# A hybrid convolution and S5 encoder block on one core: the convolution moved in between the last SSM batches, and the out-projection's halves in the other order

## The chip, the cores and the metric

One core of one Trainium2 chip runs the whole block. The metric is the device time of the kernel in microseconds (us); the kernel before takes 2246.47 us, the median of three runs.

## What is computed

The input is one sequence of 2048 vectors of 1024 channels, in front of which 16 learned meta tokens are put. The block is, with everything in float32:

```
p = rms_norm(h) @ w_in          # columns: 512 conv value, 512 conv gate, 512 S5 input
conv = silu(layer_norm(depthwise_conv31(value * sigmoid(gate)) + conv_b))
s5   = glu(gelu(S5(input) + D * input))   # 32 groups x 16 channels, 64 complex states, 2 directions
h = h + concat(conv, s5) @ w_out
h = h + relu(rms_norm(h) @ w_ff1)**2 @ w_ff2
out = rms_norm(h) without the meta positions
```

## The kernel before

The 2048 tokens are cut into 16 tiles; tile t holds the tokens 16c + t, c = 0..127, and four tiles make a block (blk = 0..3). A large matrix product is done in split precision: each operand is a high and a low part, and `mm3` (L150) issues three 512-column matmuls (L151, L152, L153) for one product. So a "unit" of the in-projection, one gate, value or u output of 128 channels for one block, is 8 x 3 = 24 matmuls.

The order of the program is the order of priority for a scheduler that fills each engine's list: an instruction written earlier goes first if its operands can be there, and later ones fill the gaps. The stages in that order are:

1. In-projection of blocks 0 and 1 and the parameters of the SSM, up to about 236 us.
2. The SSM, `ssm_run(b)` for b = 0..15 (L722), each batch a pair of groups. In a batch TensorE forms `v` from the loaded `u` (8 matmuls, L733); DVE turns it with phasors (`r`, `zi`), scans it in both directions (L751, L752) and turns it back (`s`, `st`); TensorE then makes `y` from `u` with `mt` and from `st` with `pc` (16 matmuls, L766, L769), and ACT writes it to DRAM (`ydr`). `ssm_prep(b + 3)` (L644) makes the matrices of a later batch: `pb`, its transposes `tr_wb` and `wb`, `pc`, the local kernel `k` and, by way of DRAM (`gdr`), `mt`. The in-projection of blocks 2 and 3 (`do_u`, `do_gv`, L283 and L296) is written after or among the batches and fills TensorE between their steps.
3. The convolution, `conv_quad(q)` for q = 0..15 (L824), each 32 channels. SP loads a `u8` of 260 KB (L829) from `vdr`, where the gated value was written, and four `cb` of 192 KB (L833), the banded filter; each `cb` meets three 128-column matmuls (L835), and DVE adds the bias into four blocks `cv` (L840). There are two `u8` and six `cb` buffers. All these loads stand in the one in-order queue of SP.
4. The out-projection. `s5_out(blk)` (L878) loads `y`, forms gelu, the GLU (`glu`, 48 matmuls per block) and `wout_mm(0, blk)`; then `ln_out(blk)` (L907) takes the layer norm of `cv` (16 BN_STATS at L911 over all blocks, a normalise, transposes `tr_ln`, `lzz`, a split `zc` whose low part is made on POOL) and `wout_mm(1, blk)` (L853) multiplies by the other half of w_out. Each `wout_mm` reads the residual from DRAM and writes it back: the first half x to `pdr`, the second `pdr` to `hdr`.
5. The feed-forward part, in which TensorE never rests, to the end.

Four slots of 16 KB per partition, `zslot` (L76), hold the normalised blocks z (high and low parts of two at a time) and later the split w_out (`woh`, `wol`) and the FFN's z2.

Of the kernel before, what the change touches and what calls it, by code (L numbers as in the profile page):

```python
# [1 line left out]

# [35 lines left out]
def hymba_kernel(ctx, tc, x, meta, norm_mix_g, w_in, conv_w, conv_b, conv_ln_g, conv_ln_b,  # L38
# [72 lines left out]
    def rsqrt(src, n, scale, name):  # L111
        """1 / sqrt(scale * src + eps), src [P, n]."""
        a, y, t, u = (consts.tile([P, n], F32, tag=f"rs_{q}{n}", name=f"rs{q}_{name}", bufs=2) for q in "aytu")
        tsc(a, src, scale, ALU.mult, EPS, ALU.add)
        rsqrt_steps(y, a, t, u)
        return y

    def rsqrt_steps(y, a, t, u):
        """y = a^-1/2: a guess from the exponent, a Newton step, a step of third order"""
# [4 lines left out]
        stt(u, t, -3.0, y, ALU.add, ALU.mult)         # -2 y  # L124
# [29 lines left out]

    with ExitStack() as es2:
# [45 lines left out]
        # ---------------- in-projection  # L201
# [22 lines left out]
        def load_split(src, name, hot=True, meta=False):  # L224
            """src: [1024, 128] of a weight -> hi / lo tile [P, 2, (k, col)]; the meta tokens' part of the product."""
# [21 lines left out]
        def meta_mm(r, n, name):  # L247
            """[(quarter of k, token), n]: parts of the product of the meta tokens"""
# [8 lines left out]
        def meta_cols(name):  # L257
            """[P, 16], in PSUM: the columns of the meta tokens"""
# [24 lines left out]
        def do_u(half, j, w=None, blks=None, ps=None):  # L283
            if w is None:
                w = u_weights(half, j, meta=(half == 0))
            for blk in blks or (2 * half, 2 * half + 1):
# [4 lines left out]
                with tc.high_priority():  # L291
                    st = stage(j, blk, umeta, f"stu{j}_{blk}")
                    S.copy(out=st[:, :, 1:W - 1], in_=ps.rearrange("p (s c) -> p s c", s=4))
                    flush(S, st, j, blk, udr)

        def do_gv(half, j, by_block=False):  # L296
# [25 lines left out]
            for f, blk in ([(f, blk) for blk in blks for f in (gate, value)] if by_block  # L322
                           else [(f, blk) for f in (gate, value) for blk in blks]):
                f(blk)

        def cmul(o, a, b, t0, t1):
            """complex product of APs given as (re, im)"""
# [7 lines left out]
        with (tc.tile_pool(name="pp", bufs=1, reuse_waits="tile") as PP,  # L335
# [4 lines left out]
            # ---------------- SSM parameters, [(dir, p), g]  # L340
# [31 lines left out]
            def sincos(so, co, th):  # L372
# [16 lines left out]
                # quadrant  # L389
# [25 lines left out]
            def pview(o, nr, n):  # L415
                """[P, part, batch, g, n]; parts: re, im, then sums"""
# [3 lines left out]
            pha, phb = pview(448, 3, 10), pview(508, 4, 13)      # Q^(13 a), Q^b  # L420
# [8 lines left out]
            def ssm_load():  # L429
# [14 lines left out]
                # C  # L444
# [16 lines left out]
                # D on the diagonal  # L461
# [7 lines left out]
            def ssm_params():  # L469
# [12 lines left out]
                # f = (lambda - 1) / lam  # L482
# [18 lines left out]
                # powers of lambda  # L501
# [12 lines left out]
                # rho = |lambda|^16  # L514
# [4 lines left out]
                # Q = unit phasor of lambda^16 (conjugate for the reverse direction)  # L519
# [50 lines left out]
                # the forward states are read two columns on: Q^-2  # L570
# [18 lines left out]
            # ---------------- convolution  # L589
# [25 lines left out]
            do_u(0, 0, uw[0], (0,), ps0)  # L615
            do_u(0, 1, uw[1], (0,))
# [3 lines left out]
            for j in range(2):  # L620
                do_u(0, j, uw[j], (1,))
            load_cols()
            ssm_load()
            do_u(0, 2)
            do_u(0, 3)
# [3 lines left out]
        with (tc.tile_pool(name="pb", bufs=1, reuse_waits="tile") as PB,  # L629
# [14 lines left out]
            def ssm_prep(b):  # L644
# [4 lines left out]
                def pv(o, nr, n):  # L649
                    """[P, part, g, n]"""  # L650
# [5 lines left out]
                def outer(o_re, o_im, a, b4, la, lb, on=V):  # L656
                    """complex products of a and b4, laid out by la and lb, from three real ones"""
# [17 lines left out]
                # W_b: [(h, s'), g, half of h, ri, (dir, p)]  # L675
# [41 lines left out]
                # phasor tables  # L717
# [60 lines left out]

            for j in range(4):
                do_gv(0, j, by_block=(j == 3))  # L780
# [6 lines left out]
            for j in range(2):  # L787
                do_u(1, j, uw[j], (2,))
# [3 lines left out]
            for j in range(2):  # L792
                do_u(1, j, uw[j], (3,))
            for b in range(16):
# [10 lines left out]
        # ---------------- convolution, S5 output, out-projection  # L805
        gB = consts.tile([P, D], F32, tag="gvec", name="gffn", bufs=1)
        SP.dma_start(gB, norm_ffn_g[0].partition_broadcast(P))
        with tc.tile_pool(name="p3", bufs=1, reuse_waits="tile") as P3:
# [3 lines left out]
            convb = t3([P, 512], "convb")  # L812
            SP.dma_start(convb, conv_b[0].partition_broadcast(P))

            cv = [t3([P, 4, 512], f"cv{blk}") for blk in range(4)]
# [3 lines left out]
            def hl_tile(name):  # L819
                if not hlp:  # L820
                    hlp.append(es3.enter_context(tc.tile_pool(name="p3b", bufs=1, reuse_waits="tile")))
                return hlp[0].tile([P, 2, 512], F32R, tag="hl", name=name, bufs=9)

            def conv_quad(q):  # L824
                """channels 32 q .. 32 q + 31"""
                j = q // 4
                ps = ks_ps(f"cv{q}", [P, 4, NT, 8])
                u8 = t3([P, 4, W], f"u8_{q}", bufs=2, tag="u8")
                SP.dma_start(u8, dap(vdr[j], (q % 4) * 32 * NT * W, [[W, P], [P * W, 4], [1, W]]))  # L829
                for i in range(4):  # L830
                    g8 = 4 * (q % 4) + i
                    cb = t3([P, 384], f"cb{q}_{i}", tag="cb", bufs=6)
                    SP.dma_start(cb, dap(edr[j], g8 * 8 * 504, [[504, 8], [8, 16], [1, 384]]))  # L833
                    for m in range(3):
                        T.matmul(ps[:, i].rearrange("p t c -> p (t c)"), u8[:, i, 2 - m:2 - m + P], cb[:, ts(m, P)],  # L835
# [256 lines left out]
```

## Time and profile before

| | us |
|---|---|
| median of 3 runs (lowest, highest) | 2246.47 (2242.87, 2249.4) |
| span of the profiled execution | 2244.0 |
| PE busy / DVE busy / ACT busy / POOL busy | 2143.7 / 1311.7 / 552.5 / 158.3 |
| SSM batches, first v to last v | 236.7 to 450.5 |
| end of the in-projection | about 496 |
| convolution, first to last matmul | 496.2 to 582.4 |

The profile gives no time for the execution beside its span; the span lies between the lowest and the median of the runs. The busy time of PE is 96% of the span, but that is an average: it holds a feed-forward stage of 1400 us at 100%. The stages to read for this change lie between 236.7 and 850 us.

### The profile page before, as it was taken

Reading aid. Unit: us, or ns where it says so; the run is one execution under the profiler, and the core shown is the slowest. Engines: PE = TensorE matmul, PEld = TensorE weight load, DVE = VectorE, ACT = ScalarE, POOL = GpSimd, SP = SyncE. Lnnn points to the kernel's source line nnn. Section 1 sums busy time; section 2 is a strip of 40 time slices with the busy share of each in tenths; the row PEclk is TensorE's granted clock in tenths of the full one; section 3 lists DMA queues with packets and bytes.
Section 4 is the critical chain, followed back from the end, with each engine's and each line's share of the span. In section 5 each row is a group of like instructions: output and inputs, shape, how many; then the busy total and the mean of one; then the engine's idle time right before and its main releaser. Section 6 shows DMA issues by size and latency. Waiting matters only on the chain.

```text
span 2244.0 us, 26522 instructions
## 1 busy us (share of the span) xinstructions
PE 2143.7 (96%) x10508; PEld 1750.8 (78%) x10508; DVE 1311.7 (58%) x2399; ACT 552.5 (25%) x886; POOL 158.3 (7%) x240
## 2 busy tenths in 40 slices
PE   7989888898999999999999999999999999999998
PEld 5767777776777778888888888888888888888886
DVE  6866799952676555554444454469544444554456
ACT  5323222230233222112212211234122122112212
POOL 1031344400002100000000000000000000000000
PEclk9999999999999999999999999999999999999999
DMA  6245344356543574111111111225111111112102
GB/s 189 92 163 184 114 116 126 115 172 201 163 140 114 201 260 135 47 38 62 52 38 57 47 47 40 64 66 186 59 59 55 38 57 48 47 39 63 50 19 75
DMA packets 189955, 215.37 MB, mean 96 GB/s; under 512 B 19789, under 2 KB 153433, under 8 KB 189320
## 3 DMA queue, kind: packets, MB, share of 16 engines
q1 hardware_dynamic: 174696, 199.89, 28.4%
q10 hardware_dynamic: 13856, 9.54, 1.4%
q0 software_dynamic: 1280, 4.26, 0.5%
q8 instruction: 82, 1.34, 0.3%
q14 instruction: 41, 0.34, 0.0%
HBM read 168.65 MB, written 45.01 MB: 95 GB/s over the span
## 4 chain that ended last, share of the span: by engine, by line
PE 70%; DVE 15%; DMA 6%; issue 3%; ACT 1%; POOL 0%; SPq 0%; ACTq 0%; DVEq 0%; POOLq 0%
PE f L151 19%; PE f L153 19%; PE f L152 19%; DMA cb<-edr 3%; PE wo L151 2%; PE wo L153 2%; PE wo L152 2%; DVE zo L752 1%; DVE acc L62 1%; DVE s L45 1%; DVE r L45 1%; DVE zo L751 1%; PE cv L835 1%; DVE k L663 1%; DVE st L45 1%
## 5 line engine op out<-in xcount | busy, mean ns | idle before, releaser
L45 DVE TENSOR_TENSOR acc<-acc,f 128x512 f32<-128x512 f32 x480 | 327.1, 687 | 252.3 <-PE f L153 252.3
L151 PE MATMUL f<-w,hid 128*128 128x512 f32 x1024 | 399.8, 390 | 0.6 <-DVE acc L45 0.5
L151 PE MATMUL f<-z2h,w 128*128 128x512 f32 x1024 | 399.3, 390 | 0.0
L152 PE MATMUL f<-w,hid 128*128 128x512 f32 x1024 | 398.9, 390 | 0.0
L153 PE MATMUL f<-z2h,w 128*128 128x512 f32 x1024 | 398.7, 389 | 0.0
L153 PE MATMUL f<-w,hid 128*128 128x512 f32 x1024 | 398.6, 389 | 0.0
L152 PE MATMUL f<-z2l,w 128*128 128x512 f32 x1024 | 398.6, 389 | 0.0
L45 DVE TENSOR_TENSOR rr<-rr 128x512 f32<-128x512 f32 x128 | 88.6, 693 | 352.2 <-ACT rr L990 352.2
L134 ACT CAST w<-raw 128x1024 fp32r<-128x1024 f32 x128 | 131.3, 1048 | 584.0 <-PE f L153 566.0
L151 PEld LDWEIGHTS f<-w,hid 128*128 128x128 f32 x1024 | 192.1, 188 | 46.8 <-DVE acc L45 3.7
L153 PEld LDWEIGHTS f<-w,hid 128*128 128x128 f32 x1024 | 192.2, 188 | 40.3
L151 PEld LDWEIGHTS f<-z2h,w 128*128 128x128 f32 x1024 | 192.2, 188 | 40.1 <-ACT z2h L134 0.2
L153 PEld LDWEIGHTS f<-z2h,w 128*128 128x128 f32 x1024 | 192.2, 188 | 39.9
L152 PEld LDWEIGHTS f<-z2l,w 128*128 128x128 f32 x1024 | 192.2, 188 | 39.7
L152 PEld LDWEIGHTS f<-w,hid 128*128 128x128 f32 x1024 | 192.2, 188 | 38.1
L990 ACT ACTIVATE rr<-f 128x512 f32<-128x512 f32 x128 | 76.5, 599 | 412.6 <-PE f L153 412.6
L135 DVE TENSOR_TENSOR w<-raw,w 128x1024 fp32r<-128x1024 f32 x128 | 154.0, 1222 | 10.8 <-ACT w L134 10.7
L135 DVE TENSOR_TENSOR hid<-rr,hid 128x512 fp32r<-128x512 f32 x128 | 88.1, 689 | 40.5 <-ACT hid L134 40.4
L134 ACT CAST hid<-rr 128x512 fp32r<-128x512 f32 x128 | 79.1, 619 | 57.5 <-DVE rr L45 57.5
L835 PE MATMUL cv<-cb,u 128*128 128x128 f32 x384 | 59.6, 295 | 18.0 <-DMA cb<-edr 14.6
L45 DVE TENSOR_TENSOR xo<-xo,wo 128x512 f32<-128x512 f32 x64 | 43.8, 684 | 52.9 <-PE wo L153 52.5
L835 PEld LDWEIGHTS cv<-cb,u 128*128 128x128 f32 x384 | 48.9, 196 | 32.4 <-DMA cb<-edr 18.0
(275 smaller groups left out, 2807.8 us busy)
## 6 DMA issues: line engine op xcount, KB each, us to landing
raw<-in_w_ff_dram SPq DMA_DIRECT2D x128, 512.0 KB
h<-hdr SPq DMA_DIRECT2D x32, 512.0 KB
cb<-edr SPq DMA_DIRECT2D x64, 192.0 KB
x<-in_x_dram SPq DMA_DIRECT2D x16, 512.0 KB
mt<-gdr SPq DMA_DIRECT2D x64, 128.0 KB
xo<-in_x_dram SPq DMA_DIRECT2D x16, 512.0 KB
pdr<-xo SPq DMA_DIRECT2D x16, 512.0 KB
xo<-pdr SPq DMA_DIRECT2D x16, 512.0 KB
```

The lines of the kernel that those rows point to most:

```text
L45: return V.tensor_tensor(out=o, in0=a, in1=b, op=op)
L62: return V.scalar_tensor_tensor(out=o, in0=a, scalar=s, in1=b, op0=op0, op1=op1)
L134: S.copy(out=hi, in_=src)
L135: on.tensor_tensor(lo, src, hi.bitcast(F32), ALU.subtract)
L151: T.matmul(ps, lh, rh, start=first, stop=False)
L152: T.matmul(ps, lh, rl, start=False, stop=False)
L153: T.matmul(ps, ll, rh, start=False, stop=last)
L663: tt(k1, la(a[:, 2]), lb(b4[:, 0]), ALU.mult)
L751: V.tensor_tensor_scan(zo[0:64, 2:4 * W + 2], f(rh)[0:64, :], f(zi)[0:64, :], 0.0, ALU.mult, ALU.add)
L752: V.tensor_tensor_scan(zo[64:128, 0:4 * W][:, ::-1], f(rh)[64:128, ::-1], f(zi)[64:128, ::-1], 0.0, ALU.mult, ALU.add)
L835: T.matmul(ps[:, i].rearrange("p t c -> p (t c)"), u8[:, i, 2 - m:2 - m + P], cb[:, ts(m, P)], start=(m == 0), stop=(m == 2))
L990: S.activation(rr, ps, AF.Relu)
```

## The change

The convolution is no longer a stage. `conv_quads(q0, q1)` does the same loads, matmuls and adds, but is called inside the loop over the SSM batches for b = 9..15, two quads each time and three at b = 12 and 15. Its output `cv` lies in two slots (`cva`, `cvb`) and its bias, its two `u8` and its six `cb` buffers in a third (`convw`), all of which held z before; its PSUM comes from the ring `mm` (two) instead of `ks` (two). For the slots to be free, the in-projection must be done: `do_u` and `do_gv` became generators, and two units (48 matmuls) are written behind each of the batches 0 to 9. The out-projection now starts with the convolution's half (`ln_out`, `wout_mm(1)`: x to `pdr`), then does the S5 half (`s5_out`, `wout_mm(0)`: `pdr` to `hdr`); the buffers of `hl` go from 9 to 16. Comments were taken out as well, which shifts the line numbers by 1 to 19.

```diff
+            rest = chain((u for j in (0,) for u in do_gv(1, j)), do_u(1, 2), (u for j in (1,) for u in do_gv(1, j)),
+                         do_u(1, 3), (u for j in (2, 3) for u in do_gv(1, j)))
             for b in range(16):
                 ssm_run(b)
                 if b + 3 < 16:
                     ssm_prep(b + 3)
-                if b in (1, 3):
-                    do_u(1, 2 + b // 2)
-            for j in range(4):
-                do_gv(1, j, by_block=(j == 3))
+                for _ in range(2):
+                    next(rest, None)
+                if b >= 9:
+                    conv_quads(16 * (b - 9) // 7, 16 * (b - 8) // 7)
...
+            def conv_quads(q0, q1):
+                if not cwork:
+                    for q in "ab":
+                        half = zslot([P, 2, 4, 512], f"cv{q}", F32)
+                        cv.extend(half[:, i] for i in range(2))
+                    cwork.append(zslot([P, 4096], "convw", F32))
+                    SP.dma_start(cwork[0][:, 0:512], conv_b[0].partition_broadcast(P))
...
+                    ps = mm_ps(f"cv{q}", [P, 4, NT, 8])
...
+                        o = 512 + 8 * W + 384 * ((4 * q + i) % 6)
+                        cb = cwork[0][:, o:o + 384]
...
             load_glu()
-            for q in range(16):
-                conv_quad(q)
-                if q == 8:
-                    load_wout(0)
-            load_wout(1)
-            for blk in range(4):
-                s5_out(blk)
+            load_wout(0)
             zcs = {0: ln_out(0)}
             for blk in range(4):
                 if blk < 3:
                     zcs[blk + 1] = ln_out(blk + 1)
-                wout_mm(1, blk, zcs.pop(blk), pdr, hdr)
+                wout_mm(1, blk, zcs.pop(blk), xv, pdr)
+            for blk in range(4):
+                s5_out(blk)
```

(`load_wout(1)` stands ahead of `load_glu()` after the change.)

Three places of the engines' lists show what this moves. TensorE around batches 14 and 15, as changed (`cv` is the convolution, its operand `convw` the third slot, `v` and `y` the steps of a batch):

```order
L741 MATMUL v14_4767<-u14_4765,wb14_4382 128x130 x8
L774 MATMUL y14_4796<-u14_4765,mt14_4426 128x128 x2
L810 MATMUL cv11_4819<-convw_4110 128x128 x12
L810 MATMUL cv12_4841<-convw_4110 128x128 x12
L777 MATMUL y14_4796<-st14_4793,pc14_4395 128x128 x2
L774 MATMUL y14_4796<-u14_4765,mt14_4426 128x128 x2
L777 MATMUL y14_4796<-st14_4793,pc14_4395 128x128 x2
L774 MATMUL y14_4796<-u14_4765,mt14_4426 128x128 x2
L777 MATMUL y14_4796<-st14_4793,pc14_4395 128x128 x2
L774 MATMUL y14_4796<-u14_4765,mt14_4426 128x128 x2
L777 MATMUL y14_4796<-st14_4793,pc14_4395 128x128 x2
L741 MATMUL v15_4865<-u15_4863,wb15_4545 128x130 x8
L774 MATMUL y15_4894<-u15_4863,mt15_4589 128x128 x2
L810 MATMUL cv13_4917<-convw_4110 128x128 x12
```

Before, the same batches had in-projection matmuls between their steps; now eight groups of three convolution matmuls stand between a batch's first two y matmuls and those that need `st`.

SP's queue as changed, where the first quads are loaded (`convw<-vdr` is a u8, `convw<-edr` a cb, `u`, `pkb` and `mt` are the loads of the SSM):

```order
L796 DMA convw_4110<-in_conv_b_dram 128x512
L803 DMA convw_4110<-vdr0_83 128x4x130
L808 DMA convw_4110<-edr0_111 128x1x384 x4
L803 DMA convw_4110<-vdr0_83 128x4x130
L808 DMA convw_4110<-edr0_111 128x1x384 x2
L735 DMA u11_4319<-udr2_81 128x4x130
L655 DMA pkb14_4373<-kdr3_94 128x612
L808 DMA convw_4110<-edr0_111 128x1x384
L723 DMA mt12_4036<-gdr12_107 128x1x256 x4
L808 DMA convw_4110<-edr0_111 128x1x384
L803 DMA convw_4110<-vdr0_83 128x4x130
L808 DMA convw_4110<-edr0_111 128x1x384 x4
```

Before, no load of the SSM stood behind one of the convolution's; now the two kinds alternate, down to the u of batch 15.

DVE from the last additions of the convolution on, before:

```order
L45 TENSOR_TENSOR cv3_4642<-cv15_5076,convb_4637 128x4x4x8
L911 BN_STATS st6_0_6093<-cv0_4639 128x6
L45 TENSOR_TENSOR gb0_2_5219<-gb0_2_5219,y0_2_5146 128x512
L912 BN_AGGR mv0_6092<-st6_0_6093 128x2
L911 BN_STATS st6_0_6093<-cv0_4639 128x6 x2
L135 TENSOR_TENSOR mhl0_2_5222<-gb0_2_5219,mhl0_2_5222 128x512
L45 TENSOR_TENSOR gb0_3_5238<-gb0_3_5238,y0_3_5157 128x512
L912 BN_AGGR mv0_6092<-st6_0_6093 128x2 x2
```

and as changed:

```order
L46 TENSOR_TENSOR cvb_4109<-cv15_4961,convw_4110 128x4x4x8 x2
L930 BN_STATS st6_0_5040<-cva_4108 128x6
L136 TENSOR_TENSOR wol1_4994<-raw_wo1_0_4995,woh1_4993 128x1024
L136 TENSOR_TENSOR wol1_4994<-raw_wo1_1_4999,woh1_4993 128x1024
L136 TENSOR_TENSOR wol1_4994<-raw_wo1_2_5003,woh1_4993 128x1024
L931 BN_AGGR mv0_5039<-st6_0_5040 128x2
L930 BN_STATS st6_0_5040<-cva_4108 128x6 x2
L931 BN_AGGR mv0_5039<-st6_0_5040 128x2
L930 BN_STATS st6_0_5040<-cva_4108 128x6
```

Before, S5 work (`gb`, `mhl`) for matmuls already under way stands among the statistics. Now all 16 BN_STATS, the low parts `wol1` of w_out and those of `gw` stand ahead of the first normalise (`cva` four times, 48 rows further down), and TensorE's next matmul after `cv15` is a transpose of its result.

## Rows read from the trace of the kernel before

**Rows 1.** The page, its head line.
```profile
span 2244.0 us, 26522 instructions
```

**Rows 2.** Windows by stage; columns in the first line.
```profile
core 0: us, PE busy (x) PEld busy (x) DVE busy (x) ACT busy (x) POOL busy (x), PEclk, DMA share, GB/s
300.00:435.00 135.00, 117.02 (x912) 98.81 (x912) 133.63 (x203) 31.78 (x61) 69.63 (x82) 1.00 0.41 120
496.00:583.50 87.50, 69.54 (x424) 54.51 (x423) 27.21 (x82) 10.78 (x16) 0.54 (x1) 0.96 0.66 203
583.50:640.00 56.50, 56.44 (x246) 44.79 (x245) 54.93 (x153) 21.97 (x36) 0.00 (x0) 1.00 0.41 139
```

**Rows 3.** Timeline of all engines, one SSM batch; start us, us, engine, line, operation, tiles.
```profile
236.66 2.06 PE L733 MATMUL v<-u,wb 128*128 128x130 f32 x16 [0.80 <-DMA u<-udr]
...
238.75 1.30 DVE L45 TENSOR_TENSOR r<-v,tab 128x520 f32<-128x520 f32 x2 [0.89 <-PE v L733]
...
244.74 1.20 DVE L45 TENSOR_TENSOR st<-s,s 128x256 f32<-128x256 f32 x2
```

**Rows 4.** Timeline of TensorE, first and last of 14 512-column matmuls.
```profile
377.68 0.39 PE L153 MATMUL g<-zh,w_g 128*128 128x512 f32 x1
...
380.71 0.40 PE L151 MATMUL g<-zh,w_g 128*128 128x512 f32 x1
```

**Rows 5.** Tile v in 440 to 470 us: the last SSM batch.
```profile
L733 PE MATMUL v<-u,wb x16: 273/275/277, 450.5 to 452.2; 128*128 128x130 f32 x16
```

**Rows 6.** Waits of TensorE from 236.7 to 496 us; total, times, longest.
```profile
PE y L769 <- DVE st L45: 12.1, 17, 1.3
PE k L697 <- DVE pc L666: 8.0, 7, 2.0
```

**Rows 7.** Tile cv; duration ns min/median/max, first and last start.
```profile
L835 PE MATMUL cv<-cb,u x384: 270/275/582, 496.2 to 582.4; 128*128 128x128 f32 x192
L45 DVE TENSOR_TENSOR cv<-cv,convb x64: 279/281/292, 502.1 to 583.3; 128x128 f32<-128x128 f32 x64
```

**Rows 8.** Waits of TensorE, 496 to 583.5 us.
```profile
PE cv L835 <- DMA cb<-edr: 14.6, 28, 2.8
```

**Rows 9.** Chain of waits, 495 to 620 us; start us, us, what.
```profile
496.33 2.91 PE cv L835 x27
...
515.48 0.95 PE cv L835 x6
516.45 6.84 DMA cb<-edr
```

**Rows 10.** Busy time per engine and granted clock, 500 to 510 us.
```profile
500.00:505.00 5.00, 2.00 (x10) 1.51 (x8) 4.67 (x8) 1.57 (x3) 0.54 (x1) 0.81 0.89 287
505.00:510.00 5.00, 4.93 (x16) 3.85 (x17) 2.37 (x7) 2.66 (x4) 0.00 (x0) 0.51 0.84 212
```

**Rows 11.** DMA view, 500 to 583 us: total, the two kinds of convolution load.
```profile
DMA packets 15914, 16.93 MB, mean 204 GB/s; under 512 B 768, under 2 KB 15360, under 8 KB 15909
...
cb<-edr SPq DMA_DIRECT2D x56, 192.0 KB
u<-vdr SPq DMA_DIRECT2D x14, 260.0 KB
```

**Rows 12.** DMA view of an SSM stretch, 300 to 396 us: GB/s in 40 slices, two loads.
```profile
GB/s 241 71 160 50 0 117 103 31 134 7 140 196 224 39 32 167 197 250 90 93 17 152 144 155 81 136 30 62 150 155 332 109 126 14 155 50 118 102 140 25
...
mt<-gdr SPq DMA_DIRECT2D x25, 128.0 KB
pkb<-kdr SPq DMA_DIRECT2D x6, 306.0 KB
```

**Rows 13.** Groups of DVE, 583.5 to 850 us; busy, mean ns, idle.
```profile
L911 DVE BATCH_NORM_STATS2 st<-cv 128x6 f32<-128x512 f32 x16 | 10.7, 677 | 0.0
...
L135 DVE TENSOR_TENSOR w<-raw,w 128x1024 fp32r<-128x1024 f32 x6 | 7.3, 1224 | 3.4 <-ACT w L134 3.2
```

**Rows 14.** The one group of POOL, same stretch.
```profile
L135 POOL TENSOR_TENSOR zc<-lzz,zc 128x512 fp32r<-128x512 f32 x16 | 22.0, 1400 | 255.4 <-ACT zc L134 255.4
```

More of the change, by code (lines that the diff above doesn't have):

```diff
@@ L1 @@
 from contextlib import ExitStack
+from itertools import chain
 import concourse.bass as bass
@@ L153, in mm3 @@
         T.matmul(ps, ll, rh, start=False, stop=last)
+    cv = []
     with ExitStack() as es2:
@@ L294, in do_u, with run @@
                     flush(S, st, j, blk, udr)
+                yield
+        def run(units):
+            for _ in units:
+                pass
         def do_gv(half, j, by_block=False):
@@ L324, in do_gv @@
                 f(blk)
+                yield
         def cmul(o, a, b, t0, t1):
@@ L614, in hymba_kernel @@
             win_mm(uw[0], 0, "u0_0", ps0, slice(256, 512))
-            do_u(0, 0, uw[0], (0,), ps0)
-            do_u(0, 1, uw[1], (0,))
+            run(do_u(0, 0, uw[0], (0,), ps0))
+            run(do_u(0, 1, uw[1], (0,)))
             z_block(1)
@@ L620, in hymba_kernel @@
             for j in range(2):
-                do_u(0, j, uw[j], (1,))
+                run(do_u(0, j, uw[j], (1,)))
             load_cols()
             ssm_load()
-            do_u(0, 2)
-            do_u(0, 3)
+            run(do_u(0, 2))
+            run(do_u(0, 3))
             ssm_params()
@@ L787, in hymba_kernel @@
             for j in range(2):
-                do_u(1, j, uw[j], (2,))
+                run(do_u(1, j, uw[j], (2,)))
             z_block(3)
@@ L792, in hymba_kernel @@
             for j in range(2):
-                do_u(1, j, uw[j], (3,))
+                run(do_u(1, j, uw[j], (3,)))
+            rest = chain((u for j in (0,) for u in do_gv(1, j)), do_u(1, 2), (u for j in (1,) for u in do_gv(1, j)),
+                         do_u(1, 3), (u for j in (2, 3) for u in do_gv(1, j)))
             for b in range(16):
@@ L810, in t3 @@
                 return P3.tile(shape, dt, tag=tag or name, name=name, bufs=bufs)
-            convb = t3([P, 512], "convb")
-            SP.dma_start(convb, conv_b[0].partition_broadcast(P))
-            cv = [t3([P, 4, 512], f"cv{blk}") for blk in range(4)]
             es3 = ExitStack()
@@ L821, in hl_tile @@
                     hlp.append(es3.enter_context(tc.tile_pool(name="p3b", bufs=1, reuse_waits="tile")))
[L822 to L835, printed above, removed]
-                                 start=(m == 0), stop=(m == 2))
-                bv = convb[:, 32 * q:32 * q + 32].rearrange("p (i c) -> p i c", c=8).unsqueeze(2)
-                for blk in range(4):
-                    o = cv[blk][:, :, 32 * q:32 * q + 32].rearrange("p t (i c) -> p i t c", c=8)
-                    add(o, ps[:, :, 4 * blk:4 * blk + 4, :], bv.broadcast_to([P, 4, 4, 8]))
+                return hlp[0].tile([P, 2, 512], F32R, tag="hl", name=name, bufs=16)
             wo = {}
@@ L904, in s5_out @@
                     mh.append(m_)
[L905 removed]
+                wout_mm(0, blk, mh, pdr, hdr)
             def ln_out(blk):
@@ L931, in ln_out @@
                 return zc
+            load_wout(1)
             load_glu()
-            for q in range(16):
-                conv_quad(q)
-                if q == 8:
-                    load_wout(0)
-            load_wout(1)
-            for blk in range(4):
-                s5_out(blk)
+            load_wout(0)
             zcs = {0: ln_out(0)}
@@ L944, in hymba_kernel @@
                     zcs[blk + 1] = ln_out(blk + 1)
-                wout_mm(1, blk, zcs.pop(blk), pdr, hdr)
+                wout_mm(1, blk, zcs.pop(blk), xv, pdr)
+            for blk in range(4):
+                s5_out(blk)
             es3.close()
```

19 lines of the change are left out of this document (17 added, 2 removed).

## The prediction

> **What bounds the kernel now.** The head line gives the time to which the sum is held [rows 1]: a span of 2244.0 us, 2.5 us (0.1%) under the median of the three runs, 2246.47; a difference of the sum is put on the median. Next I read the busy time by stage [rows 2], because the 96% of TensorE (PE) on the page is an average over stages with different limits. The reader should see three states there. From 300 to 435 us DVE works 133.6 of 135 us: the SSM batches are bound by DVE, and PE, with the in-projection as filler, has about a tenth of its time free. From 496 to 583.5 us DVE works 27 of 87.5 us and PE, by its records, 69.5: neither is the bound. From 583.5 us on PE is never idle. So only the convolution's stage has room for both engines, and what it waits for is in the chain [rows 9]: six matmul records, which are two groups of three (each 128-column matmul shows as two records), take 0.95 us, and then 6.84 us pass on loads of cb. The quads go by in (582.4 - 496.2)/16 = 5.4 us each [rows 7], where their matmuls alone, at 2.91 us for 27 records [rows 9], need 24 x 0.108 = 2.6 us. The DMA view says that 204 GB/s moved in that time [rows 11]. This is not all that the DMA engines can do: one slice of the SSM stretch shows 332 GB/s [rows 12]. It is the pace of six buffers behind one in-order queue.
>
> The idea to be priced is thus clear: loads that nothing covers go under batches that DVE bounds. What it costs is in three places.
>
> **Part 1: the in-projection squeezed into batches 0 to 9.** A batch took (450.5 - 236.7)/15 = 14.25 us from v to v [rows 3, 5]. Now two units of 24 matmuls go with each. Fourteen matmul starts stand between 377.68 and 380.71 us, 13 steps of 0.233 us [rows 4], so 48 cost 11.2 us. PE alone then needs 11.2 + y 16 x 0.216 = 3.5 + v 2.1 [rows 3] + about 1.9 for transposes and k (an estimate from the same 0.108 us per record): 18.7 us, above DVE's 14.25. But PE also waits for the loop through DVE. From the end of v (238.7 us) to the end of st (245.9 us) pass 7.2 us [rows 3]; in the new order two products for pb stand in this chain too, 0.65 us each by the two r in 1.30 us: 8.5 us, beside which PE has one unit and the transposes. After it come 14 y (3.0 us), the second unit (5.6), k (0.8) and the next v (2.1). Sum 20.0, and I take 20.1 because the low part of the next weight stands ahead of r on DVE. Lower bound 18.7 (PE never waits), upper 21 (a wait of up to 2.0 us as for k <- pc is added in part [rows 6]). Ten batches end at 236.7 + 201 = 438 us, where before v10 started at about 379. The change is 59 us late there, but owes no in-projection any more.
>
> **Part 2: batches 10 to 15 with 16 quads.** Two quads come first, 4.6 us for the seven groups ahead of v10, and their last loads stand behind those for mt12 and pkb14 in SP's queue; I put 5 us on that, one cb interval of the chain [rows 9] less what is under way, so v10 ends at about 450. For batches 10, 11 and 12, which still prepare later ones, DVE is the bound: 14.25 + 2.3 quads x 4 additions x 0.28 us [rows 7] = 16.8 us, three times 50.5. Batches 13 to 15 prepare nothing: v 2.1, the chain 7.2 with two additions in it 0.6, y 3.0: 13 us, beside which the eight groups of two quads (8 x 0.65 = 5.2 us) find room. So v15 ends at 450 + 50.5 + 26 = 526.5, its y at 537.5, cv15 and its additions at 541. For loads that are late now and then I add 2: **the convolution ends at 543 us** where it ended at 583.5. Lower bound: PE alone has 57 groups (37 us), y, v, transposes and k of six batches (41 us), so 528. Upper bound: the loads of this part are 64 x 192 KB + 16 x 260 KB = 16.8 MB for the convolution and, for the SSM, 6 times u and ydr, 3 to 4 times four mt and a pkb [rows 11, 12], about 6.8 MB; 23.6 MB at 204 GB/s are 116 us from 437 on: 553, and 565 if SP's waits (a cb waits for a slot, and the u and mt behind it wait too) add half of a cb interval per batch. I take the value near the engines' sum, since the ring now fills while PE does 8 us of other work between quads; the row nearest is the SSM stretch, whose mean load is far under its best slice [rows 12].
>
> **Part 3: the layer norm in the open.** Before, at 583.5 us, PE had glu and wo matmuls, and the stage shows PE busy 56.4 of 56.5 us while DVE works 54.9 [rows 2]: statistics, normalise and splits cost nothing there. Their cover is gone: the first matmul after cv15 is a transpose of the normalised cv. Ahead of it DVE has 16 BN_STATS (16 x 0.68 = 10.8 us), six low parts of weights (6 x 1.22 = 7.3) [rows 13], four normalises, aggregates and small steps (about 5, an estimate: the 0.28 us additions [rows 7] have a quarter of a normalise's columns); by pitch rather than duration 22 to 23. Then transposes, two DVE passes and a cast, about 3, and the low part on POOL, 1.4 [rows 14]. I take 27 us of idle PE. Lower bound 17 (the weights' low parts done earlier, as raw loads allow), upper 32 (the last three raw loads stand behind the last cb).
>
> The granted clock speaks to what follows. Before, the longest wait for cb was 2.8 us [rows 8], and in the next 5 us the clock was 0.51 of full, the lower of the two levels, 1.2 GHz, with PE busy 4.93 us [rows 10]. After an idle of 27 us I count the same again: about 6 us at half rate, 3 us lost. Lower bound 0, upper 6. The Trainium skill, TensorE: Matmul & The Clock Gate, section "Why this matters for your kernels", says to leave no PE gap of over about 3 us between bursts, or the engine drops to half clock; the rows agree at a slightly shorter gap. By that rule the new gap drops it for certain, and the sum is as I have it; without it, 3 us less.
>
> Also, two or three glu matmuls stood between quads before, 32 in all; they now come later: 32 x 0.233 = 7.5 us. Nothing else changes in number: the halves of the out-projection have the same matmuls in either order, and their DVE work is hidden under them in either order (0, with 5 either way if S5's gelu is late). One multiplier is at nothing: PSUM from the other ring, as each has two buffers.
>
> **Sum.** 543 + 27 + 3 + 7.5 - 583.5 = -3 us: 2241 for the profiled execution, **2243 us** against the median. A difference under 0.3% (6.7 us) is what a measurement of this kernel can't tell from none. So the forecast is no measurable change: 40 us are won and given back.
>
> **Rivals.**
> *Faster, batches at PE's pace.* If the ring keeps ahead everywhere and DVE's preparations slip beside the quads, part 2 ends at its lower bound, 528: 15 us less, 2228. For it: the ring is free for 8 us per batch and 332 GB/s were seen. Against: DVE had 1% of slack in these batches [rows 2] and gets the additions on top.
> *Faster, the layer norm covered.* If the scheduler's list left other matmuls for it, 27 us less, 2216; the list shows none.
> *Slower, the shared queue.* Place: SP from the first cb to the u of batch 15. A cb waits for its slot, which waits for PE, which waits for a y or v whose mt or u stands behind that cb. It decides as soon as u or mt lands later than the PE has run out of groups, that is, if the loads of a batch, 3.9 MB, take over 17 us (230 GB/s). At 204 GB/s they take 19, and part 2 ends at 553 to 558: 10 to 15 us more, 2256. For it: DMA moved no more than 204 GB/s in the only stage that had this pattern [rows 11]. Against: there the ring, not the engines, set the pace.
> *Slower, half clock among the batches.* In the SSM stretch no wait was over 2.0 us [rows 6] and the clock stayed 1.00 [rows 2]; in part 2 PE may wait 3 us or more for st or cb once per batch. If each drops the clock as at 505 us, 3 us x 6 = 18 to 20 us more: 2262. The skill's rule named above would have it so wherever the gap is long enough; no row of before shows a wait of that length there.
>
> **Chances.** The forecast 0.42, with its own range 2235 to 2252 from 20.1 +- 0.5 a batch and 27 +- 4 in the open (0.09 of it falls on faster, 0.02 on slower); PE's pace 0.22; layer norm covered 0.05; the shared queue 0.20 (0.02 of it within 0.3%); half clock 0.09; that the quads do not go between the batches at all, but run on behind batch 15 for want of slots, 0.02, about no change. So faster 0.36, same 0.35, slower 0.29. The range 2220 to 2265 takes in both neighbours with the bounds of their terms and leaves out the covered layer norm and the outer ends.
>
> **What would show it.** v10 starting near 448 and the last cv matmul near 541 (parts 1 and 2); a single gap of PE of 24 to 30 us behind it, ended by tr_ln and then by POOL's zc, with the clock at a half after it; DVE full from 450 to 500. A convolution that ends before 530 or after 553 makes the first or third rival right; a clock under 0.9 between 450 and 540 the fourth; a PE gap under 15 us the second. If all hold and the time still differs by over 10 us, the out-projection's order is what I misjudged.

## The result, and the profile after

The changed kernel takes 2265.78 us, the median of four runs (2262.98 to 2267.14), against 2246.65 for the kernel before beside it: 1.0084 of its time, with a 95% interval of 1.007 to 1.0098. It is slower, and 0.8 us outside the range. The profiled execution has a span of 2265.0 us, 21 us more than before.

The busy time by stage answers to [rows 2]; the first two rows are the SSM batches without and with quads, the third is the gap behind the convolution, the fourth the start of the out-projection, the fifth about the first 80 us of the feed-forward part:

```profile
core 0: us, PE busy (x) PEld busy (x) DVE busy (x) ACT busy (x) POOL busy (x), PEclk, DMA share, GB/s
236.00:435.00 199.00, 187.76 (x1272) 156.70 (x1272) 148.67 (x235) 43.24 (x80) 57.49 (x107) 1.00 0.40 116
435.00:556.00 121.00, 97.97 (x769) 90.67 (x767) 71.41 (x155) 15.04 (x28) 16.15 (x21) 0.92 0.61 178
556.00:584.00 28.00, 4.94 (x20) 3.64 (x21) 27.03 (x76) 7.06 (x9) 0.59 (x1) 0.54 0.35 116
584.00:640.00 56.00, 45.02 (x189) 34.43 (x189) 51.99 (x83) 24.08 (x37) 24.22 (x16) 0.86 0.36 122
830.00:910.00 80.00, 71.79 (x314) 56.66 (x313) 48.97 (x90) 27.71 (x43) 0.00 (x0) 0.96 0.54 176
```

Up to 435 us PE is nearly full (187.8 of 199 us) and the clock whole. Then PE works 98 of 121 us and DVE 71: as in the stage of before, neither is the bound. Then hardly anything runs on PE while DVE is full, and the next two stages have lost something as well.

The convolution's matmuls by tile, to be held against [rows 7], the last two columns of times being the first and the last start:

```profile
L810 PE MATMUL cv<-convw x384: 271/275/583, 434.9 to 555.0; 128*128 128x128 f32 x192
```

PE's waits in three stretches (435 to 556, 556 to 640, 830 to 910 us): in all, times, longest.

```profile
PE cv L810 <- DMA convw<-edr: 19.7, 17, 3.6
...
PE tr_ln L940 <- DVE cva L60: 21.0, 2, 20.7
PE wo L152 <- DVE xo L46: 7.2, 2, 5.8
PE tr_ln L940 <- DVE lzz L60: 3.7, 3, 1.9
...
PE trn_f L148 <- DVE h L63: 3.1, 2, 2.0
PE f L154 <- DVE w L136: 2.2, 2, 1.5
```

The loads of cb, which cost 14.6 us in a stage of their own [rows 8], cost 19.7 among the batches: moved, not hidden.

PE's timeline shows the gap itself (start, length, records; in brackets the idle time ahead and what ended it):

```profile
552.44 2.84 PE L810 MATMUL cv<-convw 128*128 128x128 f32 x24
575.99 2.06 PE L940 MATMUL tr_ln<-ident,cva 128*128 128x128 f32 x8 [20.70 <-DVE cva L60]
...
583.64 0.78 PE L152 MATMUL wo<-woh,zc 128*128 128x512 f32 x1
```

From the end of the last cv matmul (555.3 us) to the first wo matmul pass 28.3 us; counted from the start of the last cv record (555.0), as for the runs below, it is 28.6.

The feed-forward part is measured from the first start to the last start of its first product (`f<-z2h,w`), called the first and the last f here. These two tile lines and two windows over the out-projection, from before and then from the changed kernel, carry the account:

```profile
L151 PE MATMUL f<-z2h,w x1024: 387/389/499, 820.6 to 2200.7; 128*128 128x512 f32 x171
583.50:820.60 237.10, 227.69 (x1017) 179.61 (x1016) 159.91 (x322) 77.27 (x121) 21.96 (x16) 1.00 0.50 172
```

```profile
L152 PE MATMUL f<-z2h,w x1024: 387/389/777, 834.4 to 2221.6; 128*128 128x512 f32 x171
583.60:834.40 250.80, 237.70 (x1039) 189.81 (x1038) 153.78 (x261) 80.85 (x129) 24.62 (x16) 0.97 0.48 164
```

**The account.** Four distances hold the whole difference. The last cv matmul starts at 555.0 where it was 582.4: 27.4 us won. From there to the out-projection's next matmul pass 28.6 us (1.1 before, to 583.5): 27.5 lost. The out-projection, from there to the first f, takes 250.8 us (583.6 to 834.4) where it took 237.1 (583.5 to 820.6): 13.7 more, of which 10.0 are PE's busy time (237.70 against 227.69 by the windows: above all the glu matmuls that used to stand between quads, and matmuls at half clock), and 3.7 idle. From the first f to the last it takes 1387.2 us (834.4 to 2221.6) where it took 1380.1 (820.6 to 2200.7): 7.1 more. -27.4 + 27.5 + 13.7 + 7.1 = 20.9, and the spans differ by 21.0.

### The profile page after: what moved, and what is told of

Same layout as the page of the kernel before. It is cut to its first block, busy times and chain, and to the rows that moved or that the text cites. A ratio compares the mean times of both kernels' runs of the same rounds, so it can differ in the third digit from the quotient of the medians.

```text
span 2265.0 us, 26512 instructions
## 1 busy us (share of the span) xinstructions
PE 2147.0 (95%) x10508; PEld 1763.2 (78%) x10508; DVE 1304.6 (58%) x2399; ACT 551.5 (24%) x886; POOL 136.2 (6%) x240
## 4 chain that ended last, share of the span: by engine, by line
PE 75%; DVE 13%; DMA 5%; issue 2%; ACT 2%; SPq 0%; ACTq 0%; DVEq 0%
PE f L152 19%; PE f L154 19%; PE f L153 19%; PE wo L152 2%; PE wo L154 2%; PE wo L153 2%; DMA convw<-edr 2%; PE y L777 1%; PE y L774 1%; DVE acc L63 1%; DMA h<-hdr 1%; DVE s L46 1%; DVE zo L760 1%; DVE zo L759 1%; DVE st L46 1%
## 5 line engine op out<-in xcount | busy, mean ns | idle before, releaser
L810 PE MATMUL cv<-convw 128*128 128x128 f32 x384 | 57.4, 302 | 20.6 <-DMA convw<-edr 19.7
L810 PEld LDWEIGHTS cv<-convw 128*128 128x128 f32 x384 | 50.9, 208 | 26.0 <-DMA convw<-edr 23.2
```

## The experiments

All diffs are against the changed kernel, unless the text says before. Ratios are against the kernel before, beside each run.

**1. S5's half first again.** The convolution stays in the loop; only the order of the halves goes back (w_out's second part then lies in tiles of its own, and hl has 9 buffers).

```diff
-            load_wout(1)
             load_glu()
             load_wout(0)
+            load_wout(1)
+            for blk in range(4):
+                s5_out(blk)
             zcs = {0: ln_out(0)}
...
-                wout_mm(1, blk, zcs.pop(blk), xv, pdr)
-            for blk in range(4):
-                s5_out(blk)
+                wout_mm(1, blk, zcs.pop(blk), pdr, hdr)
```

> The changed kernel with the out-projection's halves in the old order (S5 half first, layer norm under it; the split w_out of the convolution's half in buffers of its own, since its slots still hold the convolution's output; nine hl buffers). Theory A (the loss is the layer norm in the open, a gap of 28 us, and the slow start of the out-projection behind it, some 16 us): the convolution ends at 555 us as in the changed kernel, the gap behind it shrinks to the preparation of the first S5 block, 8 to 12 us, and the time is 2224 to 2242, below the kernel before. Theory B (the loss is the convolution's loads and the SSM's in one queue, which ended the convolution at 555 instead of 541): the order of the halves is worth less than 8 us, 2258 or more.

Measured: 2253.89 us, 1.0045 (1.0029 to 1.0061): 12 us better than the change, and still slower than before; neither theory's figure was met. The convolution ends as late (last cv matmul 556.9), and the feed-forward part is as long (1387.0 us from the first f to the last). The gap is shorter but not closed: PE waits on S5's own start.

```profile
PE glu L152 <- ACT ghl L135: 17.0, 3, 10.2
```

So the order of the halves is part of the loss, not all of it, and the preparation of S5's first block is not covered either.

**2. The order alone.** In the kernel before, the halves are exchanged and the convolution keeps its stage.

```diff
-                    load_wout(0)
-            load_wout(1)
-            for blk in range(4):
-                s5_out(blk)
+                    load_wout(1)
+            load_wout(0)
             zcs = {0: ln_out(0)}
...
+            for blk in range(4):
+                s5_out(blk)
```

> The kernel before with nothing but the halves of the out-projection exchanged (convolution's half first; the convolution stays a stage of its own behind the SSM). Theory A: the layer norm loses its cover here too, 26 us of gap plus some 14 us of slow start plus the 7 us of glu matmuls that stood between the quads: 2280 to 2300. Theory B: at most 10 us over the kernel before, 2257 or less.

Measured: 2269.06 us, 1.0111 (1.0094 to 1.0127), between the figures of the two theories. This is the largest loss of a single edit, some 23 us for the order alone. PE has its gap here too, and the feed-forward part loses nothing (f from 848.5 to 2227.2 us, 1378.7).

```profile
PE tr_ln L921 <- DVE cv L59: 14.2, 3, 12.8
```

Together with run 1: with the convolution in its stage the order costs some 23 us; with it in the loop 12. That the difference is S5's start, which has lost its cover there, is a reading of run 1's waits and was not tried by itself.

**3. Without the loads of cb.** All but the first six are left out (the convolution's result is then of old filters).

```diff
-                        SP.dma_start(cb, dap(edr[j], g8 * 8 * 504, ...
+                        if 4 * q + i < 6:
+                            SP.dma_start(cb, dap(edr[j], g8 * 8 * 504, ...
```

> The changed kernel without 58 of the 64 loads of the banded filter (only the first six are loaded, later quads use what lies in the six buffers; the convolution's values are therefore left out). Theory A with the engines' sum of the forecast: the convolution ends at 541 instead of 555, 2250 to 2254. If the loads are the whole of what the batches 10 to 15 wait for, PE runs at its own pace and it ends at 528, 2238. If the waits on loads only stand beside waits on DVE, it ends at 550 or later, 2260 or more.

Measured: 2242.15 us, 0.9985 (0.9974 to 0.9997). The last cv matmul starts at 530.5, 24.5 us earlier, with PE busy 84.8 of 96 us:

```profile
435.00:531.00 96.00, 84.75 (x763) 81.66 (x761) 69.54 (x152) 15.05 (x28) 18.60 (x21) 0.98 0.38 103
```

So it is the loads that hold the end of the convolution back by these 24.5 us. The gap behind it is hardly changed (the first wo at 559.4, 28.9 us on): the two terms are independent. And even a convolution at PE's pace, with all else as in the change, only draws level with before.

**4. The loads of mt on POOL's queue.** The convolution's loads stand behind those of mt in SP's queue, and mt waits there for the write of g to DRAM. SP's waits of the changed kernel, 420 to 560 us:

```profile
SPq L808 <- DMA convw<-edr: 13.9, 12, 2.6
SPq L723 <- DMA gdr<-g: 11.1, 3, 4.5
```

```diff
-                        SP.dma_start(mt[:, g, half, :],
+                        GP.dma_start(mt[:, g, half, :],
```

> The changed kernel with the four loads of mt per batch issued from POOL's queue, so that a cb never stands behind an mt that waits for gdr. Theory B (head of SP's queue): the gap of 7 us at 439 to 450 us goes and smaller ones later, the convolution ends at 543 to 548, 2253 to 2259. Theory A says nothing about it beyond that the gap behind the convolution stays 28 us. If the pace of the DMA engines and of the ring of six is what counts, no change: 2262 to 2268.

Measured: 2254.35 us, 1.0049 (1.0032 to 1.0066), 11 us less than the change. The quads run from 431.7 to 544.4 us, and the gap stays, 28.9 (first wo 573.3). The volume of the loads is the same in both. So 11 of the 24.5 us of run 3 come from mt's place in SP's queue, where it had three waits of 3.7 us on average at the head.

**5. The hl buffers at the other end of memory.** The feed-forward part's loss had no cause in its code. By the two programs' memory maps (in KB of 1000 bytes) the hl pool of the change, now of 16 buffers and lower down since cv has left its place, covers 143.5 to 209 KB of a partition; the feed-forward's w2 lies at 159.9 to 184.4 and h6 behind it; before, hl started at 191.7 KB. A cast of a feed-forward weight waits on ACT until the last wo matmul has read hl:

```profile
813.37 1.04 ACT L135 CAST w<-raw 128x1024 fp32r<-128x1024 f32 x1
832.56 1.05 ACT L135 CAST w<-raw 128x1024 fp32r<-128x1024 f32 x1 [18.15 <-PE wo L154]
```

The edit gives hl 9 buffers at the top end, clear of the first w2 and of h6.

```diff
-                    hlp.append(es3.enter_context(tc.tile_pool(name="p3b", bufs=1, reuse_waits="tile")))
-                return hlp[0].tile([P, 2, 512], F32R, tag="hl", name=name, bufs=16)
+                    hlp.append(es3.enter_context(tc.tile_pool(name="p3b", bufs=1, side="right", reuse_waits="tile")))
+                return hlp[0].tile([P, 2, 512], F32R, tag="hl", name=name, bufs=9)
```

> The changed kernel with nine hl buffers again, at the top of the memory, where they lay before, instead of sixteen lower down. Theory C (found in the traces, not in the prediction: hl now lies where the feed-forward part wants its first w2 and its first h, so their casts and loads wait for the last matmul of the out-projection, and ACT and DVE stand behind them): the stalls of TensorE from 830 to 905 us, about 7 us of gaps and half clock, go; 2256 to 2261. If those stalls come from the late end of the out-projection itself, no change: 2263 to 2268. If seven buffers fewer hold back the layer norm, slower: over 2268.

Measured: 2258.37 us, 1.0059 (1.0042 to 1.0075), 7.4 us less than the change. The weights' low parts on DVE (between 760 and 850 us, first and last start) are made in time again: three from 835.2 on, behind the first f, in the change; five from 817.2 on in this run.

```profile
L136 DVE TENSOR_TENSOR w<-raw,w x3: 1216/1218/1220, 835.2 to 845.5; 128x1024 fp32r<-128x1024 f32 x3
```

```profile
L136 DVE TENSOR_TENSOR w<-raw,w x5: 1219/1224/1228, 817.2 to 836.1; 128x1024 fp32r<-128x1024 f32 x5
...
830.00:910.00 80.00, 78.62 (x358) 63.79 (x357) 44.43 (x78) 25.59 (x41) 0.00 (x0) 1.00 0.52 173
```

From the first f (832.9) to the last (2211.6) now pass 1378.7 us: all of the 7.1 is back.

**6. The low parts of weights on POOL.** Six of DVE's 1.22 us passes stand in the gap; POOL is idle there.

```diff
-                    split(hi[:, k, :], lo[:, k, :], r)
+                    split(hi[:, k, :], lo[:, k, :], r, GP)
```

(and the same for gw.)

> The changed kernel with the ten low parts of w_out and of the glu weight on POOL instead of DVE. Theory A (the gap of 28 us is DVE's own line of work, 8 us of it for six low parts; the four later ones cause the stall of 5.8 us at 627 and its half clock): gap 20 to 22 us, stall gone, 2250 to 2257. If the gap is set by the raw weights landing late (gw was cast at 564 to 565 us), the gap stays above 25 us and the gain is the stall alone, 2258 to 2262. If POOL beside DVE slows both (the products lzz by lsg took 1.18 us beside POOL, 0.69 us alone), no gain: 2263 or more.

Measured: 2265.84 us, 1.0099 (1.0084 to 1.0114): nothing won; 29.5 us from the last cv matmul (552.9) to the first wo (582.4). DVE is rid of 7.3 us, but some of its smallest operations became far longer beside POOL's passes. One of them on DVE's timeline of the change:

```profile
567.98 0.16 DVE L59 TENSOR_SCALAR rst_ln<-rsa_ln 128x4 int32<-128x4 int32 x1
```

and in this run, below the first four passes of POOL from POOL's timeline:

```profile
554.35 9.37 POOL L136 TENSOR_TENSOR wol<-raw_wo,woh 128x1024 fp32r<-128x1024 f32 x4 [55.95 <-DVE cvb L46]
...
559.09 2.23 DVE L59 TENSOR_SCALAR rst_ln<-rsa_ln 128x4 int32<-128x4 int32 x1
561.24 0.68 DVE L930 BATCH_NORM_STATS2 st<-cva 128x6 f32<-128x512 f32 x1
561.84 1.90 DVE L60 TENSOR_SCALAR rsy_ln<-rst_ln 128x4 int32<-128x4 int32 x1
```

Five such steps took 1.14, 2.23, 1.90, 1.96 and 2.22 us, some 8.7 us more than the 0.7 that the same five take in the change, while the BN_STATS between them kept their 0.68 us. So the run does not say whether DVE's weights are in the way: what leaves DVE for POOL comes back in the chain.

**7. Layer norm of block 0 ahead of the weights.** The same suspicion, met by order instead of by engine.

```diff
-            load_wout(1)
...
-            zcs = {0: ln_out(0)}
+            with tc.high_priority():
+                zcs = {0: ln_out(0)}
+            load_wout(1)
```

> The changed kernel with the layer norm of block 0 written, and given priority, ahead of the loads of w_out and of the glu weight, so that on DVE eight BN_STATS of other blocks come behind the normalise of block 0 instead of ahead of it. Theory A (the gap of 28 us is the length of DVE's line up to that normalise): gap 22 to 24 us, 2259 to 2263. If the gap is set by the last raw weights (their low parts are still ahead of the normalise), it stays at 27 us or more and the time at 2264 or more.

Measured: 2259.69 us, 1.0064 (1.0048 to 1.0081), 6 us less than the change; the gap is 22.9 us (553.6 to 576.5). But the weights' low parts did not go behind: on DVE's timeline four of wol (the first at 558.10) and two of gw still stand ahead of the first normalise (cva).

```profile
558.10 1.22 DVE L136 TENSOR_TENSOR wol<-raw_wo,woh 128x1024 fp32r<-128x1024 f32 x1
...
567.72 1.22 DVE L136 TENSOR_TENSOR gw<-raw_gw,gw 128x1024 fp32r<-128x1024 f32 x1
568.87 1.91 DVE L60 TENSOR_SCALAR cva<-cva,mv,rsy_ln 128x512 f32<-128x512 f32 x4
...
570.77 0.68 DVE L930 BATCH_NORM_STATS2 st<-cvb 128x6 f32<-128x512 f32 x1
```

What went behind it are statistics of other blocks: 9 of the 16 BN_STATS stand ahead of the normalise now, where all 16 did. So the statistics of later blocks, at 0.66 us each, stood in the chain; the 22.9 us that remain still hold the six low parts, 7.3 us of DVE, and no run took them out without a price.

**8. Three units of the in-projection per batch,** so that the quads start at b = 7.

```diff
-                for _ in range(2):
+                for _ in range(3):
...
-            if b >= 9:
-                conv_quads(16 * (b - 9) // 7, 16 * (b - 8) // 7)
+            if b >= 7:
+                conv_quads(16 * (b - 7) // 9, 16 * (b - 6) // 9)
```

> The changed kernel with three units of the in-projection behind a batch instead of two, so that it is done after batch 6, and the convolution from batch 7 on (nine batches for sixteen quads instead of seven). Theory B' (the loads need more time than seven batches give: 24 us of the stretch go when they are left out): SSM and convolution together end at 532 to 542 instead of 556, 2244 to 2254. If TensorE's work alone sets the stretch, they end within 5 us of 556: 2260 or more.

Measured: 2272.46 us, 1.0123 (1.0106 to 1.014): worse by 7 us. The quads start 20 us earlier and end 10 us later (415.3 to 564.6), as more batches that still prepare mt now have cb in the same queue; from 380 to 570 us SP waits on the write of g for 35.7 us, where it waited 20.1 in the change:

```profile
SPq L723 <- DMA gdr<-g: 20.1, 5, 4.6
```

```profile
SPq L723 <- DMA gdr<-g: 35.7, 8, 6.3
```

**9. The same with mt on POOL's queue** (the edits of runs 4 and 8).

> Three units per batch with the convolution from batch 7 on, as in the run that came out slower, and the loads of mt on POOL's queue. Theory B'' (what made three units slower is that mt of batches 10 to 15 stood in SP's queue among the cb: eight waits for gdr, 36 us in all, with six of them at new places): without these waits nine batches give the loads room, SSM and convolution end at 528 to 540, below the 545 us of mt on POOL with two units; 2238 to 2250. If the pace of the loads themselves sets the stretch, they end at 545 or later, 2254 or more.

Measured: 2259.35 us, 1.007 (1.0049 to 1.0092), 13 less than run 8 and 5 more than run 4. Theory B'' missed; the other branch, with an end at 545 us or later, is what came. With mt away from SP the quads end at 548.1, and still later than with two units. Where the last 4 us come from was not settled; PE waits 13.5 us on st and POOL's queue 48.1 us on g in that stretch.

**10. The mended parts in the order of the change:** three units, mt on POOL, hl at the top, layer norm first (the edits of runs 4, 5, 7 and 8).

> A combination with the convolution's half first: three units per batch, mt on POOL's queue, nine hl buffers at the top, layer norm of block 0 first. Sum from the changed kernel, 2265.8: minus 11 (mt), minus 7 (hl), minus 4 (layer norm first), minus 4 to 14 (three units): 2230 to 2240. If the stretch does not end earlier than 545 us: 2243 to 2247.

Measured: 2250.59 us, 1.0014 (1.0001 to 1.0027). With these four mended and the convolution's half still first it is about level with before, and slower than both of its forecasts.

**11 to 14. The other order, with cover.** S5's half first, mt on POOL, hl and w_out's second part at the top end, w2 laid ahead of hid in the feed-forward part, and the last three quads written behind the loop, beside which ACT and DVE make S5's first ghl. Of the edit, the quads:

```diff
-                conv_quads(16 * (b - 9) // 7, 16 * (b - 8) // 7)
+                conv_quads(13 * (b - 9) // 7, 13 * (b - 8) // 7)
+            conv_quads(13, 16)
```

> A combination: the changed kernel with mt loaded from POOL's queue (11 us there), the S5 half first, three of the sixteen quads kept for behind batch 15 as cover for the preparation of the first S5 block (the gaps of 10.5 and 5.5 us of the run with the S5 half first), hl and the convolution's w_out at the top of the memory and w2 laid ahead of hid in the feed-forward part (some 5 us). Sum from the run with the S5 half first, 2253.9: minus 11, minus 12, minus 5: 2220 to 2234, which is 0.6 to 1.1% below the kernel before. If loads, gap and memory overlap in what they cost, 2236 to 2246.

Measured: 2244.85 us, 0.9997 (0.9987 to 1.0007), in the weaker of the two forecasts. The first f stands at 814.7, but from there to the last f it takes 1385.1 us, 6 more than in run 5: here h6 lies under w_out's second part. The next version puts h6 at the bottom end, has three units, and loads w_out behind the first ghl:

> A combination with the S5 half first: as the first combination, with three units per batch, with h6 laid at the bottom of the feed-forward part's memory (there its load waited for the last matmul of the out-projection and held back the next weights, 6 us of stalls at 815 to 880 us), and with the splits of w_out behind the first S5 preparation on DVE. From 2244.9: minus 5 to 6, minus 4 to 10 for three units, minus 2 to 4 for the splits: 2226 to 2234. If the end of the convolution does not move: 2236 to 2241.

Measured: 2234.07 us, 0.995 (0.9932 to 0.9968). The same with two units:

> The third combination (S5 half first, three quads kept behind batch 15, mt on POOL's queue, memory laid out so that the feed-forward part waits for nothing of the out-projection, splits of w_out behind the first S5 preparation) with two units per batch instead of three. If moving the convolution is worth its loads once its side costs are gone, and three units cost what they did in the runs with them (5 us between mt on POOL with two and with three): 2226 to 2231. If the first glu, at 565 us there, does not come earlier: 2233 to 2236.

Measured: 2229.83 us (2224.24 to 2232.75), 0.9921 (0.9905 to 0.9937), 17.5 us under the kernel before beside it. Its stages, to be read against the last three rows of the changed kernel's (the first f stands at 808.8 here, so the last row begins 21 us behind it):

```profile
556.00:584.00 28.00, 25.55 (x97) 19.18 (x98) 27.77 (x44) 19.94 (x31) 0.00 (x0) 0.90 0.49 157
584.00:640.00 56.00, 56.00 (x243) 44.38 (x243) 49.24 (x140) 17.48 (x28) 0.00 (x0) 1.00 0.49 165
830.00:910.00 80.00, 79.16 (x354) 65.27 (x353) 44.19 (x69) 18.23 (x28) 0.00 (x0) 1.00 0.34 112
```

Not all of the 17.5 us is the convolution's. By the two traces the first f comes 11.8 us earlier than before (808.8 against 820.6), and from there to the last f it takes 1375.2 us, 4.9 less than the 1380.1 of before; this version lays the feed-forward part's buffers out differently too, and the kernel before was not run with that layout alone.

The last run takes the cover away from that version: all 16 quads in the loop again.

> The same with all sixteen quads inside the loop, none kept behind batch 15. If the quads behind batch 15 cover the preparation of the first S5 block, the gap ahead of the first glu is 9 to 12 us at half clock after it instead of 5: 4 to 8 us over the run with cover, 2231 to 2238. If the loads of these quads cost as much as they cover, the two are within 3 us.

Measured: 2236.46 us, 0.9952 (0.9937 to 0.9966), 6.6 us more. PE's waits from 540 to 640 us, with the three quads behind the loop and then without, and the window from 556 to 584 us without:

```profile
PE glu L152 <- ACT ghl L135: 6.4, 2, 5.9
```

```profile
PE glu L152 <- ACT ghl L135: 11.2, 3, 9.5
...
556.00:584.00 28.00, 24.46 (x76) 16.50 (x77) 26.95 (x51) 18.82 (x29) 0.00 (x0) 0.77 0.37 114
```

Without cover the longest wait is 3.6 us longer and the clock behind it 0.77 instead of 0.90; the first f comes at 813.8, 5.0 us later. In these two traces the feed-forward part is 3.7 us longer as well (1378.9 against 1375.2); whether that belongs to the cover was not settled.

## Why the prediction was wrong

The sum said -3 us, the trace +21. By the prediction's own terms:

- **What bounds the kernel, and part 1: right.** The in-projection was to end at 438 us and ended at 434.7, at 20.0 us a batch from v1 (254.5) to v9 (414.8). One reading was too wide: that PE is never idle from 583.5 us on holds to 640; up to the first f it was idle 9.4 of 237.1 us.
- **Part 2 failed: 543 us was 555.** The sum of the engines' work was taken as the bound, with 2 us "for loads that are late now and then". The v of batches 10, 13 and 15 show where it went wrong, with the windows between them and, last, the window from v13 to v15 of run 3:

```profile
444.02 2.05 PE L741 MATMUL v<-u,wb 128*128 128x130 f32 x10
494.82 1.96 PE L741 MATMUL v<-u,wb 128*128 128x130 f32 x16
540.25 1.96 PE L741 MATMUL v<-u,wb 128*128 128x130 f32 x16
...
444.00:494.80 50.80, 41.83 (x332) 39.02 (x331) 33.73 (x67) 6.69 (x14) 11.86 (x16) 0.88 0.64 184
494.80:540.30 45.50, 36.23 (x279) 32.74 (x278) 27.34 (x62) 4.24 (x9) 3.75 (x4) 0.92 0.64 188
```

```profile
482.50:515.40 32.90, 30.14 (x276) 29.03 (x275) 25.54 (x60) 4.34 (x9) 3.75 (x4) 1.00 0.44 116
```

  Batches 10 to 12 took 50.8 us, 50.5 forecast, but by luck: DVE, which was to bound them, worked 33.7 of these. Batches 13 and 14 took 45.5 us, 26 forecast. Without the loads they take 32.9, and PE alone works 30.1 of them: the 13 us a batch, taken from DVE's chain, were too short even for PE's own work, and the loads add the other 12.6. Over the whole stretch the last cv matmul stands at 530.5 in run 3, near the prediction's lower bound of 528 and 10 us under its sum, and with the loads 24.5 us later.

  The rival with the shared queue had the right place and the right figure (553 to 558). The chain it gave is not what the trace shows: no wait of PE from 435 to 556 us is for u or mt, and 19.7 us are for cb, so the loads of the convolution are late, not those that stand behind them. Run 4 shows a wait in the opposite direction, cb behind an mt that waits for g (11 us); that the remaining 13 are the volume of the loads was not tried. The reason to set this rival behind, that the ring fills while PE works between quads, did not save PE from these 17 waits.
- **Part 3: right in its sum.** 28.3 us in the open, 27 forecast, though not as one gap: 20.7 us up to tr_ln, where 24 to 30 were named, then 7.6 of transposes and short waits, where the parts came to 4.4. PE's busy time in the out-projection grew by 10.0 us, 10.5 forecast for glu and half clock. What the prediction did not do is ask whether this belongs to the move or to the order. Run 2 answers: the order alone loses some 23 us.
- **"Hidden under them in either order (0, with 5 either way)" failed by 3.7 us,** inside its bounds. At 626.8 PE waits 5.8 us for the addition of a residual, because three low parts of S5's w_out stand ahead of it on DVE:

```profile
626.33 5.63 DVE L136 TENSOR_TENSOR wol<-raw_wo,woh 128x1024 fp32r<-128x1024 f32 x3
631.89 1.87 DVE L46 TENSOR_TENSOR xo<-xo,wo 128x512 f32<-128x512 f32 x3
```

- **"Nothing else changes in number" failed by 7.1 us.** Moved buffers change what later ones lie on, which no list of instructions shows. It was no term at all; run 5 gives all of it back.
- **Half clock among the batches: happened, and was no term.** The clock is 0.92 from 435 to 556 us, and 0.98 in run 3 without the loads (435 to 531). By these two means 8% of 121 us and 2% of 96 are missing, so at most some 8 of the 24.5 us of run 3 are matmuls at the lower rate (an estimate); how much of it lies on the path is open, since faster matmuls would have waited for the same loads. The rival put it at 18 to 20. After two idle stretches of PE, 3.52 us from 439.1 on and 3.65 from 446.1, the next 5 us were at the lower level, 1.2 GHz, with PE full:

```profile
450.00:455.00 5.00, 5.00 (x24) 5.00 (x25) 2.19 (x6) 0.58 (x1) 0.00 (x0) 0.50 0.63 200
```

The rule of the Trainium skill cited in the prediction (TensorE: Matmul & The Clock Gate, "Why this matters for your kernels") would have it so at these lengths, and this row agrees.

The misses add up, part 2 taken to the end of its last matmul (555.3): 12.3 for part 2, 1.3 for the gap, 3.7 - 0.5 for the out-projection and 7.1 for the memory are 23.9, against 21.0 + 3.

## What to carry to other kernels

A stage with idle engines may be what covers the next one's start: before it is filled elsewhere, list what runs beside it, and leave enough behind (with three quads of sixteen the first f came 5.0 us earlier here). A load that waits for a write holds all loads behind it in an in-order queue, so try it in a queue of its own before others are mixed in (11 us here). And when a buffer moves, look at what the next stage puts on that address, since a cast that waits there holds its whole engine (7 us).

## What the runs showed of the hardware

Beside POOL's passes over 128x1024 (2.34 us each, 1.21 for the same pass on DVE), five of DVE's steps on 128x4 elements took 1.14 to 2.23 us where they take 0.14 to 0.16 alone (run 6). Each of the five ended within 0.03 us of the end of a pass of POOL (at 558.99, 561.30, 563.72, 566.20 and 568.50 us), so they were held up to that end and not merely slowed. BN_STATS and BN_AGGR beside the same passes kept their times (0.66 to 0.68 and 0.14 to 0.17 us). So handing work to an idle POOL can lengthen a chain of small DVE steps by more than it takes away.
